# Five row tiles in the first norm instead of three, their weights' low parts by a subtraction on GpSimd instead of an accumulating DMA

## Chip, cores and metric

The kernel runs on one core of a Trainium2 chip. The metric is the device time of one execution in microseconds (us). Five engines work side by side, each in its own program order: TensorE (PE; PEld is its weight loading), VectorE (DVE), ScalarE (ACT), GpSimd (POOL) and SyncE (SP), which here only issues DMAs. ACT and POOL issue some DMAs too.

## What is computed

Two transformer blocks on 512 tokens of 1024 channels, all in float32. The part that matters here is the start of the first block, its first layer:

```python
mod = silu(c) @ ada_w[0] + ada_b[0]
shift, scale, gate = jnp.split(mod, 3, axis=-1)
h = rms_norm(x, norm_g[0]) * (1.0 + scale) + shift
z = h @ even_w_in                       # 1024 x 7296
a_val, a_glu, a_gate, r, k, v, wd, ad, b_gate = split_cols(z, EVEN_SIZES)
ya = conformer_conv(a_val, a_glu, ...) * silu(a_gate)
yb = rwkv7_mix(r, k, v, wd, ad, ...) * silu(b_gate)
x = x + gate * (concat(ya, yb) @ even_w_out)
```

After it come an attention layer, a short-convolution and pooling mixer, a layer with 16384 experts (choose the best 16 for each of 8 heads, then all experts' products), and a last gated projection.

## The kernel before

Channels lie on the 128 partitions, tokens along the free dimension: `x0` to `x7` are 128 x 512 tiles. A projection's output is worked in row tiles of 128 channels; `in_wev` holds 57 of them for `even_w_in`. Tile 48 is the low-rank inputs `wd` and `ad`, tiles 24 to 31 are `r`, 32 to 39 `k`, 40 to 47 `v`, 8 to 15 `a_glu`, 0 to 7 `a_val`.

To keep float32 accuracy each operand is split into a high and a low part, and `product` (L214 to L218) does three matmuls for each of the 8 pieces of 128 input channels: high x high (L216), high weight x low input (L217), low weight x high input (L218). A row tile is thus 24 matmuls into one PSUM bank. `weight` (L179) delivers the parts. In the first layer it loads a piece of 512 columns as `draw` (SP), copies it on ACT to `dh` (L190), copies it negated to `dl` (L191), and adds the same weights to `dl` by a second, accumulating DMA that POOL issues (L192). `draw` has 3 buffers, `dh` and `dl` 4.

`first_norm` (L313) makes `h`. The scales and shifts come from `in_adaT`: 16 loads `adaw` of 512 KB, each multiplied with `cond` and summed on DVE (L349), followed by small DVE instructions on `mod` and `gs` (L351, L352). For each j of 8, POOL makes `xr` = x times the reciprocal root mean square (L347), ACT applies scale and shift (L354) and makes the high part `xh` (L355), DVE the low part `xl` (L356), and PE adds the j-th three matmuls of every row tile in the tuple `FIRST` to its bank. When the norm ends, the tiles of `FIRST` lie complete in `self.ready`; `wev` hands them out, and projects any other tile with `proj`.

Behind it `even` runs the steps of `ORDER`: A0 A1 d c0 A2 B0 C0 B1 ... `A` (`rwkv_a`) makes the operands of two heads: ACT and DVE instructions on `r`, `k`, `v`, `sig`, `a`, `kk` up to `BK`, then 16 matmuls L620 and `MT`. `d` is the gate of the layer (`gate`, L423): 16 loads `pr` of 256 KB in two buffers, each reduced on DVE (L437). `c` is a convolution tile: 12 matmuls L774 whose operands use the buffers of `pr` again. `B` inverts small triangles: SP writes `MT` out as `Ld` (L647) and reads it back as `Lp` (L651), then 31 steps `Ltmp` (L660) and `Tp` (L662), then a transposition (L675) and matmuls L680. `C` is the recurrence over 8 chunks, each beginning with L702.

PSUM has 8 banks: `mm` 3 (two and one of `psum2`), `tp` 2, `xu` 2, `nb` 1. `xu` is used by `B` and `C`.

The order of instructions on each engine is set by a planner, the class `Order` (L1555): it has a price for each instruction, simulates the engines' queues by list scheduling from several priorities, and imposes the order that comes out shortest by its own prices on the whole program. A change at the start can thus move instructions everywhere. SP's loads in `first_norm` and of the gate are chained in the order in which they are written (`follow`).

Of the kernel before, what the change touches and what calls it, by code (L numbers as in the profile page):

```python
# [10 lines left out]
F32 = mybir.dt.float32  # L11
F32R = mybir.dt.float32r
# [7 lines left out]
T = 512  # L20
# [113 lines left out]
class Net:  # L134
# [178 lines left out]
    def first_norm(self, hi, lo):  # L313

        nc = self.nc
        mod, gs = self.mod[0], self.gs[0]
        with self.tc.tile_pool(name="ada", bufs=1) as pool:
            cond = pool.tile([128, 1024], F32, name="cond")
            loads = self.loads = []
# [7 lines left out]
                load(self.x[j], self.I["xT"][:, j])  # L327
            load(self.vec, self.I["vec"])
            def parts(i):
                for k in range(0, 1024, self.KR * 128):  # L330
                    yield from self.weight(self.I["wev"][i][:, k:k + self.KR * 128], loads)
            first = [(i, parts(i)) for i, _ in self.FIRST]
            ws = {}
            nc.scalar.activation(crow, crow, AF.Silu)
# [4 lines left out]
            rs = self.rstd(pool, self.x)  # L339
            self.ready = {i: self.bank(b) for i, b in self.FIRST}  # L340
            for j in range(8):
# [32 lines left out]
                                               op0=OP.mult, op1=OP.add)  # L374

    AW = 16
    FIRST = ((48, "mm"), (32, "mm"), (24, "mm"))
    WB, RB, KP, KR = 8, 6, 2, 2
    wd, DR, DB = None, 3, 4
    GB = 3  # L380
# [1520 lines left out]
```

## Time and profile before

| | us |
|---|---|
| median of 3 runs | 2843.48 (2837.21 to 2843.74) |
| the profiled execution | 2849.02 |
| its span, first to last instruction | 2847.1 |
| PE busy in the span | 2638.1 (93%) |
| DVE busy | 2125.0 (75%) |
| POOL busy | 1722.0 (60%) |
| ACT busy | 1467.5 (52%) |

The busy shares are averages over stages that have different limits. The first layer takes the first 780 us or so; the change touches its first 60 us directly. A row of the timeline begins with the start in us and the duration in us; what stands in brackets at its end is the engine's idle time before it and what ended that.

### The profile page before, as it was taken

The page shows a single profiled execution, that of the slowest core. Times are in us where ns is not written, and L with a number is a line of the kernel's source. Part 1 is how long each engine was busy: PE and PEld are TensorE (multiplying, and loading weights), DVE is VectorE, ACT ScalarE, POOL GpSimd, SP SyncE. Part 2 cuts the span into 40 slices and gives each one's busy share as a digit, 9 for nine tenths or more (in the row PEclk, how much of TensorE's full clock was granted, in tenths as well). Part 3 has the DMA queues.
Part 4 walks back from the last instruction along what each step waited for, and adds up shares of the span by engine and source line. Part 5 has one row for each costly group of instructions (what it writes and reads, how often), then busy time and mean ns, then how long its engine had stood idle before and what let it go on. Part 6 is the DMA issues. An engine that isn't in the chain of part 4 may idle for free.

```text
span 2847.1 us, 45547 instructions
## 1 busy us (share of the span) xinstructions
PE 2638.1 (93%) x14715; PEld 2209.6 (78%) x14715; DVE 2125.0 (75%) x4274; ACT 1467.5 (52%) x3135; POOL 1722.0 (60%) x1862
## 2 busy tenths in 40 slices
PE   5899999999979899999999978789999999999996
PEld 3666666666666678877888767789999999999995
DVE  6667657666459998963669999767787777788775
ACT  6646645557546348965453358533344334334435
POOL 4423512221255443346657688779999899898963
PEclk9879999999989999999999999989999999999998
DMA  8744444565783221223334366899999999999972
GB/s 268 163 91 95 96 103 104 108 136 128 174 284 98 69 80 51 77 72 107 94 106 133 112 194 248 309 327 333 319 333 330 331 327 327 326 320 337 328 244 77
DMA packets 353442, 552.26 MB, mean 194 GB/s; under 512 B 60081, under 2 KB 239153, under 8 KB 351538
## 3 DMA queue, kind: packets, MB, share of 16 engines
q1 hardware_dynamic: 224690, 295.22, 32.5%
q0 software_dynamic: 64800, 201.88, 23.9%
q10 hardware_dynamic: 63712, 52.24, 5.8%
q8 instruction: 116, 1.90, 0.3%
q14 instruction: 124, 1.02, 0.1%
HBM read 507.76 MB, written 41.42 MB: 193 GB/s over the span
## 4 chain that ended last, share of the span: by engine, by line
PE 59%; DVE 21%; DMA 6%; issue 5%; POOL 4%; ACT 3%; ACTq 0%; SPq 0%; DVEq 0%; POOLq 0%
PE mm L218 11%; PE mm L217 11%; PE mm L216 11%; PE xu L1254 2%; PE xu L1252 2%; PE xu L1253 2%; DVE x L778 2%; PE mm L774 2%; DVE o L1507 1%; DVE Ltmp L660 1%; DVE Tp L662 1%; PE tp L1254 1%; POOL wl L209 1%; PE tp L1253 1%; PE tp L1252 1%
## 5 line engine op out<-in xcount | busy, mean ns | idle before, releaser
L209 POOL TENSOR_TENSOR wl<-wraw,wh 128x256 fp32r<-128x256 f32 x937 | 759.3, 828 | 392.5 <-ACT wh L207 302.4
L207 ACT ACTIVATE wh<-wraw 128x256 fp32r<-128x256 f32 x937 | 368.3, 412 | 498.0 <-PE mm L217 256.7
L216 PE MATMUL mm<-xh,wh 128*128 128x352 f32 (+1 forms) x1464 | 512.2, 352 | 28.9 <-ACT wh L207 12.5
L218 PE MATMUL mm<-xh,wl 128*128 128x352 f32 (+1 forms) x1464 | 507.5, 351 | 13.7 <-POOL wl L209 13.4
L217 PE MATMUL mm<-xl,wh 128*128 128x352 f32 (+1 forms) x1464 | 509.6, 350 | 2.1 <-DVE xl L287 2.0
L216 PEld LDWEIGHTS mm<-xh,wh 128*128 128x128 f32 x1464 | 279.7, 191 | 53.0 <-ACT wh L207 15.9
L218 PEld LDWEIGHTS mm<-xh,wl 128*128 128x128 f32 x1464 | 278.6, 191 | 38.2 <-POOL wl L209 19.7
L217 PEld LDWEIGHTS mm<-xl,wh 128*128 128x128 f32 x1464 | 279.8, 191 | 23.0 <-DVE xl L287 4.5
L192 POOL DMA_DIRECT2D dl<-in_wev x114 | 100.9, 893 | 300.4 <-ACT dl L191 223.9
L1236 POOL TENSOR_TENSOR vl<-vraw,vh 128x1024 fp32r<-128x1024 f32 x96 | 232.3, 2421 | 5.6 <-ACT vh L1232 4.4
L1357 DVE SCALAR_TENSOR_TENSOR wide<-grow,gdot,wide 128x1024 f32<-128x1024 f32 x158 | 202.7, 1283 | 20.2 <-DMA grow<-in_ev,gidx 18.5
L1341 DVE SCALAR_TENSOR_TENSOR gscr<-grow,wide 128x1024 bf16<-128x1024 f32 x160 | 194.2, 1214 | 19.1 <-DMA grow<-in_ue,gidx 17.4
L216 PE MATMUL mm<-xh,dh 128*128 128x512 f32 x456 | 198.2, 437 | 10.6 <-ACT xh L355 10.0
L217 PE MATMUL mm<-xl,dh 128*128 128x512 f32 x456 | 194.1, 428 | 8.8 <-DVE xl L356 8.8
L218 PE MATMUL mm<-xh,dl 128*128 128x512 f32 x456 | 192.9, 425 | 6.0 <-DMA dl<-in_wev 6.0
L1326 POOL DMA_INDIRECT grow<-in_ue,gidx x160 | 163.6, 1022 | 56.3 <-issue 17.5
L1326 POOL DMA_INDIRECT grow<-in_ev,gidx x160 | 159.8, 999 | 39.6 <-issue 20.3
L1187 ACT ACTIVATE mm<-mm 128x352 f32<-128x352 f32 x96 | 43.0, 448 | 262.7 <-PE mm L218 257.7
L1254 PE MATMUL xu<-wwh,vl 128*128 128x352 f32 x512 | 167.2, 327 | 9.1 <-POOL vl L1236 9.1
L1252 PE MATMUL xu<-wwh,vh 128*128 128x352 f32 x512 | 166.1, 325 | 7.9 <-DVE x L1256 6.2
L1253 PE MATMUL xu<-wwl,vh 128*128 128x352 f32 x512 | 165.6, 324 | 0.0
L1232 ACT ACTIVATE vh<-vraw 128x1024 fp32r<-128x1024 f32 x128 | 134.4, 1053 | 50.3 <-DMA vraw<-in_ev 39.0
(573 smaller groups left out, 6762.8 us busy)
## 6 DMA issues: line engine op xcount, KB each, us to landing
vraw<-in_ev SPq DMA_DIRECT2D x128, 512.0 KB, 5.9
wraw<-in_uT SPq DMA_DIRECT2D x494, 128.0 KB, 4.5
draw<-in_wev SPq DMA_DIRECT2D x114, 256.0 KB, 3.2
dl<-in_wev POOLq DMA_DIRECT2D x114, 256.0 KB, 4.8
gs<-st SPq DMA_DIRECT2D x11, 2048.0 KB, 7.7
g<-gs ACTq DMA_DIRECT2D x32, 704.0 KB, 9.6
wraw<-in_wod SPq DMA_DIRECT2D x156, 128.0 KB, 2.2
adaw<-in_adaT SPq DMA_DIRECT2D x32, 512.0 KB, 7.2
```

Of the source, the lines that this page charges most:

```text
L207: nc.scalar.activation(wh, raw[:, s], AF.Copy)
L209: nc.gpsimd.tensor_tensor(wl, raw[:, s], wh.bitcast(F32), OP.subtract)
L216: nc.tensor.matmul(ps, wh, xh, start=start, stop=False)
L217: nc.tensor.matmul(ps, wh, xl, start=False, stop=False)
L218: nc.tensor.matmul(ps, wl, xh, start=False, stop=stop)
L1236: nc.gpsimd.tensor_tensor(l, raw, h.bitcast(F32), OP.subtract)
L1252: nc.tensor.matmul(po, vh[i][:, s], wh[i], start=(i == 0), stop=False)
L1253: nc.tensor.matmul(po, vh[i][:, s], wl[i], start=False, stop=False)
L1254: nc.tensor.matmul(po, vl[i][:, s], wh[i], start=False, stop=(i == len(wh) - 1))
L1326: self.nc.gpsimd.indirect_dma_start(out=t, out_offset=None, in_=src, in_offset=bass.IndirectOffsetOnAxis(ap=self.gidx[i][:, k:k + 1], axis=0))
L1341: nc.vector.scalar_tensor_tensor(scr, u, 1.0, x, op0=OP.mult, op1=OP.mult, accum_out=self.gdot[i][:, k:k + 1])
L1357: nc.vector.scalar_tensor_tensor(acc, r, w, acc, op0=OP.mult, op1=OP.add)
```

## The change

`FIRST` gets two more tiles, 40 (`v` of step A0) and 8 (`a_glu` of step c0), which accumulate in the two `xu` banks. The weights of all five are no longer delivered by `weight`, but in `first_norm` itself: a piece of 512 columns is loaded as `fraw`, ACT copies it to the high part `fh`, and POOL subtracts, `fl` = `fraw` - `fh`. Each of the three names has five buffers, so the second half of a tile's weights goes into the buffers of its first half. Ten loads take the place of six loads and six accumulating DMAs; ten copies on ACT that of twelve; ten POOL subtractions of 128 x 512 are new.

```diff
             def parts(i):
-                for k in range(0, 1024, self.KR * 128):
-                    yield from self.weight(self.I["wev"][i][:, k:k + self.KR * 128], loads)
+                for k in range(0, 1024, T):
+                    raw = pool.tile([128, T], F32, name="fraw", bufs=len(self.FIRST))
+                    load(raw, self.I["wev"][i][:, k:k + T])
+                    wh, wl = (pool.tile([128, T], F32R, name=n, bufs=len(self.FIRST)) for n in ("fh", "fl"))
+                    self.split(wh, wl, raw, nc.gpsimd)
+                    for c in range(0, T, 128):
+                        yield wh[:, c:c + 128], wl[:, c:c + 128]
...
-    FIRST = ((48, "mm"), (32, "mm"), (24, "mm"))
+    FIRST = ((48, "mm"), (32, "mm"), (24, "mm"), (40, "xu"), (8, "xu"))
```

`split` (L239) is the helper that was there: a copy on ACT and a subtraction on the engine given. Lines after L330 are five higher in the changed kernel.

On POOL, the stretch of the first norm up to the first instruction of step A0. Before:

```order
L192 DMA dl<-in_wev 128x512 x3
L347 ISA
L347 TENSOR_TENSOR xr<-x_76,rs 128x512
L347 TENSOR_TENSOR xr<-x_77,rs 128x512
L347 TENSOR_TENSOR xr<-x_78,rs 128x512
L347 TENSOR_TENSOR xr<-x_79,rs 128x512
L347 TENSOR_TENSOR xr<-x_80,rs 128x512
L347 TENSOR_TENSOR xr<-x_81,rs 128x512
L347 TENSOR_TENSOR xr<-x_82,rs 128x512
L192 DMA dl<-in_wev 128x512
L347 TENSOR_TENSOR xr<-x_83,rs 128x512
L192 DMA dl<-in_wev 128x512 x3
```

Now:

```order
L242 TENSOR_TENSOR fl<-fraw,fh 128x512 x5
L352 TENSOR_TENSOR xr<-x_76,rs 128x512
L352 TENSOR_TENSOR xr<-x_77,rs 128x512
L352 TENSOR_TENSOR xr<-x_78,rs 128x512
L352 TENSOR_TENSOR xr<-x_79,rs 128x512
L352 TENSOR_TENSOR xr<-x_80,rs 128x512
L352 TENSOR_TENSOR xr<-x_81,rs 128x512
L352 TENSOR_TENSOR xr<-x_82,rs 128x512
L352 TENSOR_TENSOR xr<-x_83,rs 128x512
L242 TENSOR_TENSOR fl<-fraw,fh 128x512 x5
L192 DMA dl<-in_wev 128x512 x4
```

Five subtractions stand ahead of the eight `xr` and five behind them, where accumulating DMAs stood.

On DVE, in step A0, from `sig` to `kk`. Before:

```order
L584 TENSOR_SCALAR sig<-sig 128x512
L592 SCALAR_TENSOR_TENSOR cu<-scan,sig 128x512
L593 TENSOR_TENSOR sig<-cu,sig 128x512
L546 SCALAR_TENSOR_TENSOR r<-mm,om,tm 128x512
L590 TENSOR_SCALAR rsq<-nb 128x512
L602 SCALAR_TENSOR_TENSOR kk<-k,vec,rsq 128x512
```

Now:

```order
L589 TENSOR_SCALAR sig<-sig 128x512
L597 SCALAR_TENSOR_TENSOR cu<-scan,sig 128x512
L598 TENSOR_TENSOR sig<-cu,sig 128x512
L442 SCALAR_TENSOR_TENSOR pr,gpart<-pr,cs 128x512
L442 SCALAR_TENSOR_TENSOR pr,gpart<-pr,crs 128x512
L595 TENSOR_SCALAR rsq<-nb 128x512
L551 SCALAR_TENSOR_TENSOR r<-mm,om,tm 128x512
L442 SCALAR_TENSOR_TENSOR pr,gpart<-pr,cs 128x512
L442 SCALAR_TENSOR_TENSOR pr,gpart<-pr,crs 128x512
L442 SCALAR_TENSOR_TENSOR pr,gpart<-pr,cs 128x512
L607 SCALAR_TENSOR_TENSOR kk<-k,vec,rsq 128x512
```

Five reductions of the gate stand between `sig` and `kk` (before there were two further up, ahead of this piece).

On SP, the loads around the first `Ld` (step B0). Before:

```order
L569 DMA wup<-in_wup 64x2x128 x2
L186 DMA draw<-in_wev 128x512
L434 DMA pr<-in_adaT 128x512 x2
L186 DMA draw<-in_wev 128x512 x2
L434 DMA pr<-in_adaT 128x512 x2
L647 DMA Ld<-MT 32x16x32 x2
L434 DMA pr<-in_adaT 128x512 x2
L651 DMA Lp<-Ld 32x1024 x4
```

Now:

```order
L439 DMA pr<-in_adaT 128x512 x6
L186 DMA draw<-in_wev 128x512 x3
L439 DMA pr<-in_adaT 128x512
L574 DMA wup<-in_wup 64x2x128 x2
L439 DMA pr<-in_adaT 128x512
L186 DMA draw<-in_wev 128x512
L439 DMA pr<-in_adaT 128x512 x4
L652 DMA Ld<-MT 32x16x32 x2
L439 DMA pr<-in_adaT 128x512 x2
L656 DMA Lp<-Ld 32x1024 x4
```

`Ld` stood behind 8 of the 16 loads of `pr` and stands behind 14.

## Rows read from the trace of the kernel before

**Rows 1.** Busy us (count) by stretch: PE, PEld, DVE, ACT, POOL; clock, DMA share, GB/s.

```profile
0.00:60.00 60.00, 31.72 (x82) 19.58 (x83) 43.81 (x87) 36.62 (x56) 26.21 (x39) 0.94 0.87 285
60.00:120.00 60.00, 44.35 (x201) 34.40 (x199) 41.33 (x85) 44.85 (x75) 27.86 (x45) 0.91 0.80 186
160.00:200.00 40.00, 39.75 (x256) 25.26 (x255) 29.21 (x77) 11.40 (x31) 5.95 (x10) 0.62 0.38 78
200.00:300.00 100.00, 97.16 (x591) 60.09 (x590) 58.86 (x147) 56.04 (x127) 28.34 (x47) 0.97 0.47 95
```

**Rows 2.** Waits from 0 to 60 us: us in total, times, longest.

```profile
PE mm L217 <- DVE xl L356: 8.8, 4, 6.0
DVE xl L356 <- ACT xh L355: 4.5, 3, 1.9
```

**Rows 3.** Timeline of PE: two neighbours at 53 us, two at 60 us.

```profile
52.94 0.63 PE L217 MATMUL mm<-xl,dh 128*128 128x512 f32 x1
53.37 0.63 PE L218 MATMUL mm<-xh,dl 128*128 128x512 f32 x1
...
60.55 0.39 PE L216 MATMUL mm<-xh,dh 128*128 128x512 f32 x1
60.78 0.39 PE L217 MATMUL mm<-xl,dh 128*128 128x512 f32 x1
```

**Rows 4.** Timeline of DVE in the first norm, ahead of and beside POOL's `xr`.

```profile
17.01 0.15 DVE L352 SCALAR_TENSOR_TENSOR gs<-mod,vec 128x1 f32<-128x1 f32 x1
...
18.55 1.22 DVE L349 SCALAR_TENSOR_TENSOR adaw<-adaw,cond 128x1024 f32<-128x1024 f32 x1
...
19.69 1.21 DVE L352 SCALAR_TENSOR_TENSOR gs<-mod,vec 128x1 f32<-128x1 f32 x1
...
20.93 2.27 DVE L349 SCALAR_TENSOR_TENSOR adaw<-adaw,cond 128x1024 f32<-128x1024 f32 x1
```

**Rows 5.** Tile `xr`: POOL's durations in ns (min/median/max), first and last start.

```profile
L347 POOL TENSOR_TENSOR xr<-x,rs x8: 1257/2017/2315, 19.2 to 33.6; 128x512 f32<-128x512 f32 x8
```

**Rows 6.** DMA queues from 0 to 60 us: packets, MB, share of 16 engines.

```profile
q1 hardware_dynamic: 6194, 15.00, 68.3%
q0 software_dynamic: 1008, 1.84, 17.3%
```

**Rows 7.** Timeline, step A0: DVE's `kk` and PE's first L620.

```profile
72.27 0.75 DVE L602 SCALAR_TENSOR_TENSOR kk<-k,vec,rsq 128x512 f32<-128x512 f32 x1 [4.89 <-ACT rsq L600]
...
79.04 2.32 PE L620 MATMUL tp<-AR,BK 64*128 64x128 f32 x16 [3.79 <-DVE BK L612]
```

**Rows 8.** Chain that ended last: start, us, what; waits for `pr`, three of five.

```profile
81.04 2.66 DMA pr<-in_adaT
...
84.52 6.17 DMA pr<-in_adaT
...
107.00 4.55 DMA pr<-in_adaT
```

**Rows 9.** Timeline, steps A1, c0, B0, C0: SP, PE, PE, DVE, PE, PE.

```profile
89.26 0.87 SPq L647 DMA_DIRECT2D Ld<-MT  x2
...
116.16 1.71 PE L620 MATMUL tp<-AR,BK 64*128 64x128 f32 x16
...
145.06 4.46 PE L774 MATMUL mm<-u,pr 128*128 128x512 f32 x10
...
158.22 0.87 DVE L675 STREAM_TRANSPOSE T<-Tt 32x256 f32<-32x256 f32 x2
...
162.93 1.09 PE L680 MATMUL xu<-T,MT 32*32 32x32 f32 x32
...
209.86 0.34 PE L702 MATMUL xu<-UV,MT 128*64 128x64 f32 x4
```

**Rows 10.** The choice of experts: busy us by stretch, and a wait from 1440 to 1860 us.

```profile
1520.00:1540.00 20.00, 20.00 (x110) 17.95 (x109) 20.00 (x104) 7.65 (x19) 15.71 (x19) 1.00 0.39 118
...
PE mm L216 <- ACT wh L207: 12.2, 3, 7.4
```

## The prediction

> **What bounds the kernel now.** I read the busy times by stage first. From 200 to 300 us PE is busy 97.16 of 100 us, and from 160 to 200 us 39.75 of 40, there at a granted clock of 0.62 on average [rows 1]: in the first layer PE sets the pace once it runs. In the first 60 us it is busy 31.72, in the next 60 us 44.35 [rows 1]: some 44 us in which it waits. The waits of the first norm come next: PE waits 8.8 us for `xl` from DVE, and DVE only 4.5 us in three waits for `xh` [rows 2]. So DVE's queue of scales paces the first norm. The timeline of DVE then shows what slows DVE there, and the chain of waits, from 80 us on, that the gate's `pr` loads pace steps A0 and A1 [rows 8]. The reader is to see two things: there is idle PE time to put work into, and DVE, which must feed that work, has none to spare.
>
> **Matmuls moved into the idle time.** Tiles 40 and 8 are 48 matmuls of 512 columns. Neighbours start 0.43 us apart at 53 us and 0.23 us apart at 60 us [rows 3]; this is the level of the clock. At the faster pitch 48 are 11.0 us. They stood behind the first norm, between 60 and 120 us. Counted in the orders of PE: ahead of A0's first L620 stood 122 of these matmuls and stand 175; ahead of A1's first L620 197 and 235; when c0's 12 convolution matmuls and A1's L620 are all issued, 240 and 240. So PE carries a lead of 53 matmuls (12.2 us) to A0 and of 38 (8.7 us) to A1, and at the end of c0 both kernels have done the same work. What counts is when that point is reached.
>
> **Subtractions on GpSimd.** Ahead of POOL's `xr` a small DVE instruction on `gs` takes 0.15 us and a sum over `adaw` 1.22 us; beside them the same take 1.21 and 2.27 us [rows 4]. Each loses 1.05 us to one POOL instruction, and POOL's own grow from 1.26 us (smallest) to 2.02 us (median) [rows 5]: the two engines go by turns. Eight `xr` make eight such stops. Ten subtractions of the same shape are added. The first two run before the first scales have landed and stop nobody; I take eight stops, 8.4 us, less about half of DVE's 4.5 us of waits [rows 2], which a later DVE shortens: the first norm ends 6 us later. Bounds: 0 (three stops, all absorbed by the waits) and 12 (ten stops and the 1.4 us by which scales land later, below).
>
> **DMA and ACT.** In the first 60 us the POOL queue's 1.84 MB, which are eight accumulating transfers, cost 17.3% of 60 us on all 16 engines, 1.30 us each; SP's 15.00 MB cost 68.3%, which is 0.72 us for 256 KB [rows 6]. Six accumulations less and four loads more are 4.9 us less DMA time. Nothing on the path waits for it, since DVE is short of time and not of scales; I count 0. In the other direction, five loads instead of three stand ahead of the first scales: at 0.72 us each, the scales land up to 1.4 us later (in the bound above). ACT does two copies fewer there; it is not the limit.
>
> **The gate's loads.** Now five reductions of `pr` stand between `sig` and `kk` on DVE. `pr` has two buffers, so each pair waits for a load that starts when the pair before is done; before, five such waits lay on the chain, 2.66, 6.17 and at last 4.55 us among them [rows 8], 4.4 us in the mean. Before, DVE was free for `kk` at 67.4 (72.27 less the 4.89 us of waiting for ACT [rows 7]), and `sig` was done 1.4 us ahead of that, at 66; now at 72. From there the first reduction (0.7), a load (4.4), the third (0.7), a load (4.4) and the fifth (0.7) make 10.9: `kk` at 82.9, 10.6 us later than 72.27, and A0's L620 at about 90 instead of 79.04 [rows 7]. Queued behind those reductions on DVE is all of A0, and PE's next L620. On SP `Ld` stands behind 14 loads of `pr` instead of 8: issued at about 101 instead of 89.26 [rows 9]. In return the gate is done some 6 us earlier than before, and A1's part on DVE no longer shares the queue with it: A1's L620 at about 123 instead of 116.16, only 7 later.
>
> **The end of c0.** Before, 43 products and the 12 convolution matmuls follow A1's first L620, and the last convolution ends at 149.5 [rows 9]. Now 5 products and 10 convolution matmuls follow. A convolution matmul shows as two records, 0.43 us each (4.46 us for ten overlapping ones [rows 9]): 8.5 us, with 16 matmuls L620 and the transpositions 15 us. That is 138, 11 us earlier, although everything on DVE is later.
>
> **B0 and C0.** B0 starts from `Ld`, so 12 us later. Its 31 steps on DVE and POOL took from 89 to 158 us [rows 9], twice what the steps need, because A1 and the gate stood between them. A good part of the 12 us closes: I take its end 5 us later (bounds 0 and 12). C0 follows: before, its last chunk began at 209.86 [rows 9]; now at 215, but by then 12 more convolution matmuls (10.2 us) and 4 more products (0.9 us) are done. 11 less 5 is **6 us gained**. After that PE is busy 97% [rows 1], so it keeps what it has.
>
> **Sum.** 2849.0 for the profiled execution (span 2847.1 and 1.9 around it) less 6 is 2843. The median of the runs, 2843.5, lies 5.5 below the profiled one, so on that footing 2837.5: I say **2838**.
>
> **The rivals.**
> *The lead is kept in full* (A). DVE's later end is taken up by its waits, and B0's steps close all of the 12 us. Then the 11 us at the end of c0 stay, with up to 3 more if the first norm is not late: 2843.5 - 11 to - 14, 2830 to 2833. For it: B0's chain was stretched by others. Against it: DVE shows hardly any idle time in the first norm.
>
> *The lock on DVE and the gate decide* (B, slower). The place is the first norm and `kk`: all ten subtractions stop DVE, the norm ends 12 us later, `kk` 16, `Ld` 18, and B0 hands all of it to C0, whose small matmuls run at the lower clock from 160 us on [rows 1] and must wait for DVE at each chunk. C0 then ends 18 us later with 11 us more done: 7 us lost, about 2851; with a further `pr` round or a slower clock 2855. It is a loss once C0's first L702 comes more than 11 us later than before. The Trainium skill, page "SBUF — State Buffer", section "Who interferes with whom", states that a VectorE instruction with two SBUF inputs and a GpSimd instruction that reads SBUF take turns at a lock held for the whole instruction, and that whoever is second waits in full. By that rule each of the ten subtractions would cost DVE 1.26 us, 12.6 us and not 6, and the total would be about 2844 to 2851; the trace agrees on the turns, with 1.05 us for each.
>
> *The planner's other changes decide* (C). It has reordered the whole program. In the choice of experts 231 dense products stand ahead of the first one-hot transposition on PE instead of 166, 65 of some 0.16 us by my estimate from the row of 20 us with 110 matmuls [rows 10], 10 us. DVE is full there (20.00 of 20) and PE later waits 12.2 us for weights [rows 10]. If the 65 fill waits, up to 10 us are gained; if they hold up DVE's pairs, as much is lost. I count 0 in the sum.
>
> *It doesn't do what it says* (D). The second half of `fh` and `fl` reuses the first half's buffers, so tiles 40 and 8 can only go on when their first four pieces are done; if most of the 48 matmuls slip behind the last `xl`, nothing has moved into idle time. The order of PE has 24 of the 120 products from the last `xh` on, against 19 of 72 before, which speaks against it. 2843 or so.
>
> **How the numbers follow.** Forecast 0.41, A 0.22, B 0.15, C 0.14 (0.08 gained, 0.06 lost), D 0.08. A measurement of this kernel can tell about 0.3%, 8.5 us, from no change. Faster by more: A, most of C's gains and the lower end of the forecast (0.06): 0.36. Slower by more: most of B and C's losses: 0.17. Within: 0.47. The range runs from A with a little of C, 2825, to B, 2852.
>
> **What would show it.** In the changed kernel: DVE's sums over `adaw` and the small instructions at 2.3 and 1.2 us beside `fl` as beside `xr`; the last `xl` at 60 us, not 54; `kk` of A0 behind waits for `pr`, at 82; A0's L620 at 90; `Ld` at 101; the last c0 convolution at 138; the last chunk of C0 at 215 and PE busy above 95% after that. Wrong would be: a last `xl` at 54 to 56 (stops cost nothing), or one past 64; c0 ending later than 149; a C0 later by more than 11; a layer that gains and a choice of experts that gives it back.

## The result, and the profile after

The changed kernel takes 2875.75 us (median of four runs, 2871.58 to 2883.67), the kernel before 2841.33 (four runs). The ratio is 1.0119, 95% interval 1.0098 to 1.014: some 34 us **slower**, where 2838 was forecast and 2852 was the upper end of the range. The profiled execution took 2873.45 (span 2871.5), 24.4 us more than the one before (span 2847.1). The two comparisons differ because the profiled execution before lies 5.5 us above its first median and after's 2.3 below its own.

Where the 24.4 us arise is read from five stage ends that both programs have, each the last (or first) instance of a row in the timelines:

| end of stage (last or first row) | before | after | stage longer by |
|---|---|---|---|
| first layer, last `xu<-UV,MT` of the recurrence | 735.0 | 752.3 | 17.3 |
| attention and mixer, last `poolw` product | 1428.9 | 1433.8 | -12.4 |
| choice of experts, first softmax step `top<-sel` | 1667.8 | 1700.4 | 27.7 |
| to the first expert product `xu<-wwh,vh` | 1877.1 | 1882.2 | -27.5 |
| end | 2847.1 | 2871.5 | 19.3 |

The change itself touches only the first of them. Such a difference, from one execution each, is good to some 5 us: a second execution of the changed kernel (`five_again`, below) ends the first layer at 757.1 and the mixer at 1437.0, against 752.3 and 1433.8. The busy times of the first layer, where the change lies, in the kernel after; the columns are those of [rows 1] (stretch and its length, then busy us and count of PE, PEld, DVE, ACT, POOL, then clock, DMA share, GB/s):

```profile
0.00:60.00 60.00, 32.72 (x93) 21.20 (x94) 46.48 (x79) 31.57 (x47) 34.27 (x24) 0.93 0.67 248
60.00:120.00 60.00, 44.77 (x175) 34.62 (x174) 34.32 (x68) 32.98 (x56) 18.08 (x40) 0.79 0.68 172
160.00:200.00 40.00, 36.35 (x216) 26.78 (x215) 36.47 (x89) 18.30 (x35) 15.85 (x26) 0.83 0.61 133
200.00:300.00 100.00, 94.57 (x645) 56.83 (x646) 67.11 (x164) 52.97 (x133) 25.72 (x43) 1.00 0.41 85
```

In the first 60 us PE is busy one microsecond more than in [rows 1], not eleven. From 60 to 120 us it is as busy as before (44.77 and 44.35 us), but the clock granted falls from 0.91 to 0.79, and fewer instructions get done (175 and 201). DVE is idle for 26 of those 60 us. In the norm itself the waits have hardly changed, from 0 to 60 us (us in total, times, longest; [rows 2] before):

```profile
PE mm L217 <- DVE xl L361: 8.1, 4, 3.1
DVE xl L361 <- ACT xh L360: 3.2, 2, 1.6
```

DVE's timeline after says where, the columns as in [rows 4]:

```profile
43.12 1.24 DVE L357 SCALAR_TENSOR_TENSOR gs<-mod,vec 128x1 f32<-128x1 f32 x1
44.35 2.33 DVE L354 SCALAR_TENSOR_TENSOR adaw<-adaw,cond 128x1024 f32<-128x1024 f32 x1
...
59.76 0.69 DVE L361 TENSOR_TENSOR xl<-xr,xh 128x512 fp32r<-128x512 f32 x1 [1.60 <-ACT xh L360]
68.69 2.35 DVE L498 TENSOR_SCALAR om<-vec 128x25 f32<-128x25 f32 x1 [8.24 <-PE xu L218]
...
71.19 0.75 DVE L551 SCALAR_TENSOR_TENSOR r<-mm,om,tm 128x512 f32<-128x512 f32 x1
...
87.74 0.75 DVE L607 SCALAR_TENSOR_TENSOR kk<-k,vec,rsq 128x512 f32<-128x512 f32 x1
```

The last `xl` ends the norm at 60, as forecast. Then comes a wait of 8.24 us that the prediction does not have: `om`, a tiny instruction on a constant (in before at 54.17, right behind the last `xl`), waits for PE. PE's timeline shows what for, the last product with `fl`, at 68.20; under it the later steps that answer to [rows 7, 9]:

```profile
68.20 0.39 PE L218 MATMUL xu<-xh,fl 128*128 128x512 f32 x1
97.74 2.39 PE L625 MATMUL tp<-AR,BK 64*128 64x128 f32 x16
...
133.11 1.81 PE L625 MATMUL tp<-AR,BK 64*128 64x128 f32 x8 [2.62 <-DVE BK L617]
...
155.32 1.02 PE L779 MATMUL mm<-u,pr 128*128 128x512 f32 x2
...
188.35 0.48 PE L707 MATMUL xu<-UV,MT 128*64 128x64 f32 x4
...
226.05 0.34 PE L707 MATMUL xu<-UV,MT 128*64 128x64 f32 x4
```

`om` reads nothing of `fl`. But `fl` is a tile of the pool "ada", which the first norm opens and closes, and the tiles of the next phase (`om`, `hb`, `ka`, `tm` and others) take over that memory. A0's first L625 comes at 97.74, 18.7 us later than in [rows 7], and C0's last chunk at 226.05 instead of 209.86 [rows 9].

The second place is the choice of experts. DVE's timeline after, ahead of the softmax:

```profile
1669.24 0.58 DVE L1477 TENSOR_REDUCE sel<-eq 128x64 f32<-128x256 bf16 x1
...
1680.98 1.22 DVE L1346 SCALAR_TENSOR_TENSOR gscr<-grow,wide 128x1024 bf16<-128x1024 f32 x1 [3.95 <-DMA grow<-in_ue,gidx]
...
1691.46 1.22 DVE L1346 SCALAR_TENSOR_TENSOR gscr<-grow,wide 128x1024 bf16<-128x1024 f32 x1 [9.25 <-DMA grow<-in_ue,gidx]
...
1697.27 1.22 DVE L1346 SCALAR_TENSOR_TENSOR gscr<-grow,wide 128x1024 bf16<-128x1024 f32 x1 [4.58 <-DMA grow<-in_ue,gidx]
...
1700.38 0.29 DVE L1487 COPY top<-sel 128x32 f32<-128x32 f32 x1 [1.88 <-ACT grep L1293]
```

The selection is done at 1669, as good as before (1666), but `top`, the first step of the softmax, stands behind row products whose gathers have not landed: 31 us later. In before it follows at 1667.84. The plan is a trade; PE's dense products are drawn forward. The windows of this stage, the one behind it and the rest, before:

```profile
1428.90:1667.80 238.90, 222.69 (x1145) 193.01 (x1144) 211.72 (x977) 104.06 (x247) 165.78 (x201) 0.98 0.40 123
1667.80:1877.10 209.30, 159.99 (x1078) 146.21 (x1078) 177.72 (x195) 135.56 (x353) 172.93 (x144) 0.94 0.76 274
1877.10:2847.10 970.00, 928.71 (x5604) 906.94 (x5602) 734.12 (x1084) 394.26 (x811) 821.38 (x781) 0.99 0.88 304
```

and after:

```profile
1433.80:1700.40 266.60, 251.24 (x1319) 221.97 (x1318) 218.94 (x1003) 117.12 (x282) 190.39 (x234) 0.98 0.43 132
1700.40:1882.20 181.80, 127.60 (x916) 118.35 (x914) 157.10 (x154) 124.96 (x324) 149.16 (x113) 0.90 0.74 270
1882.20:2871.50 989.30, 936.55 (x5596) 912.02 (x5596) 763.84 (x1099) 393.44 (x807) 816.97 (x778) 0.98 0.87 300
```

PE's timeline after, the first expert product:

```profile
1882.19 0.66 PE L1257 MATMUL xu<-wwh,vh 128*128 128x352 f32 x1 [27.31 <-ACT wwh L241]
```

PE does 174 more products in the first stage and 162 fewer in the next. So the two stages together come out even (448.2 and 448.4). But at 1854.9 PE has no product left ahead of the first expert product, which waits for its weights `wwh`, and stands idle for 27.31 us, and the rest of the program, with the same number of products (5596 and 5604), takes 19.3 us longer.

### The profile page after: what moved, and what is told of

Read it like the earlier page. It is cut to its first block, busy times and chain, and to the rows that moved or that the text cites. A ratio compares the mean times of both kernels' runs of the same rounds, so it can differ in the third digit from the quotient of the medians.

```text
span 2871.5 us, 45542 instructions
## 1 busy us (share of the span) xinstructions
PE 2639.3 (92%) x14715; PEld 2214.1 (77%) x14715; DVE 2159.4 (75%) x4274; ACT 1457.7 (51%) x3120; POOL 1736.7 (60%) x1862
## 3 DMA queue, kind: packets, MB, share of 16 engines
q14 instruction: 123, 1.01, 0.1%
## 5 line engine op out<-in xcount | busy, mean ns | idle before, releaser
L192 POOL DMA_DIRECT2D dl<-in_wev x104 | 91.6, 890 | 279.6 <-ACT dl L191 234.0
L216 PE MATMUL mm<-xh,dh 128*128 128x512 f32 x416 | 179.8, 433 | 9.9 <-ACT dh L190 3.6
L218 PE MATMUL mm<-xh,dl 128*128 128x512 f32 x416 | 176.8, 425 | 6.9 <-DMA dl<-in_wev 6.9
L217 PE MATMUL mm<-xl,dh 128*128 128x512 f32 x416 | 176.5, 425 | 0.0
```

What stands on the lines that cost most here:

```text
L216: nc.tensor.matmul(ps, wh, xh, start=start, stop=False)
L217: nc.tensor.matmul(ps, wh, xl, start=False, stop=False)
L218: nc.tensor.matmul(ps, wl, xh, start=False, stop=stop)
```

## The experiments

Every time below is a median of timed runs beside runs of the kernel before on the same chip; the executions of before had medians of 2841.9 to 2847.9. "Five" kernels have the five row tiles of the change, "three" kernels the three of before. The planner picks one plan for the whole program, so an edit can act through the instructions that it changes or through the plan that it draws. The experiments try to hold one or the other. That does not fully succeed: a kernel whose first norm is edited anew has a first layer planned anew, also where the late order is held.

### Is it the stage of the experts?

The changed kernel with the stage of the experts and all behind it issued in the relative order that the kernel before has:

```diff
-    nc = build(A, Order(build(A)).best()[1])
+    order = hold(base, base.best()[1], other, other.best()[1], cut, ocut)
+    nc = build(A, order, Net)
```

Here `base` is the changed program and `other` the one before; from the cut on, `hold` takes the sequence of `other`.

> The changed first norm as it is; but every instruction from the stage of the experts on (choice of experts, dense products, row gathers, the end) is issued in the relative order of the kernel before, on every engine. Nothing is left out. Theory R (the planner's other order at the choice of experts costs most of the loss: the softmax over the chosen scores, top<-sel on DVE, stands behind four row products that wait for their gathers and starts 32 us later than before): the time falls from 2876 to 2844 to 2850, top<-sel starts at about 1673, that is 5 after before's 1668, the first one-hot o<-iota,kt at about 1681. Theory F (the first layer's later end, 17 us at its last chunk, is what the end pays, and the order only moves with it): the time stays at 2865 to 2876. Either way the first layer is as in the changed kernel: A0's first transposes at 97.7, the last xu<-UV,MT of the even phase at 752.

2872.27 against 2847.08, 1.0082 (1.0048 to 1.0117). The three stages went back to the lengths of before:

```profile
1448.40:1688.10 239.70, 225.15 (x1149) 194.47 (x1148) 210.49 (x977) 103.99 (x248) 165.87 (x201) 0.98 0.40 122
1688.10:1897.00 208.90, 161.28 (x1079) 148.06 (x1078) 178.33 (x194) 134.07 (x350) 172.27 (x143) 0.94 0.76 270
1897.00:2871.60 974.60, 929.30 (x5603) 907.04 (x5602) 735.11 (x1085) 394.29 (x814) 822.14 (x782) 0.99 0.89 303
```

From the last `poolw` product to the end are now 1423.2 us (1437.7 in after, 1418.2 in before). In the profiled execution the first layer ended at 762.9, ten later than in after, in nearly the same order of instructions there (ACT issues 11 DMAs less in that stretch, and some of its instructions change places). The lengths of the stages are explained by the order, the total is not: it is still 25 us over before, and most of that lies ahead of them.

The mirror image, the kernel before with the late order of after (the same `hold`, `base` and `other` exchanged):

> The kernel before up to the stage of the experts, three row tiles by the accumulating DMA; from there every instruction in the relative order of the changed kernel. Nothing is left out. The mirror of the other run. Theory R: 2865 to 2872, top<-sel some 27 to 32 us later than before's 1668. Theory F: 2838 to 2845, the same as before.

2882.45 against 2847.08, 1.0146 (1.0093 to 1.0198). The three rows answer to those of after:

```profile
1441.80:1709.60 267.80, 251.06 (x1315) 221.13 (x1314) 221.15 (x1002) 116.19 (x282) 191.04 (x234) 0.98 0.43 132
1709.60:1891.30 181.70, 128.55 (x916) 119.75 (x914) 161.87 (x154) 124.26 (x324) 147.57 (x113) 0.90 0.74 270
1891.30:2876.20 984.90, 932.80 (x5596) 909.28 (x5596) 763.02 (x1099) 392.70 (x807) 819.91 (x778) 0.98 0.88 301
```

So after's late order lengthens these stages in a kernel that has no edit at all. The total is 35 us over before, though, more than either theory said: the last `poolw` product comes at 1441.8 instead of 1428.9, ahead of the order that was changed, and why is not known. To size the late order over all kernels of this study I take the time from the last `poolw` product to the start of ACT's last output tile `yo`. Where `top` follows the last `sel` (fourteen kernels, before with 1402.1 among them) it is 1398.8 to 1413.2. With after's late order it is 1420.7, 1423.7 (after a second time) and 1418.3 (this run). This run lies 16 us over before, and after 13 over the first run (1407.6), which differ in little but this order: some 13 to 16 us. Two other late orders, of kernels below, have 1459.7 and 1459.9.

The direct test, the softmax pulled forward in the kernel before under after's late order:

```diff
+    back = key[top] - sel - 15
+    for n in chain:
+        key[n] -= back
```

> The kernel before up to the stage of the experts; from there the order of the changed kernel, but the softmax over the chosen scores, the one-hots behind it and what they need are issued as early as the last chosen index allows, as a block; the rest (dense products, gathers) keeps its order around them. Nothing is left out. Theory R (the late softmax is what that order costs): top<-sel back within 5 us of the last sel<-eq, the total at 2838 to 2852. Theory S (the rest of that order, gathers issued later and dense products issued earlier, costs as much by itself): top<-sel early, but the total stays at 2860 to 2885.

2951.36, 1.0374 (1.0351 to 1.0397). The test failed: pulling forward what the chain needs moved other instructions too, and `top` still came 27 us behind the last `sel`, now waiting for ACT. Waits on `top` in this kernel (us in total, times, longest):

```profile
DVE top L1491 <- ACT grep L1297: 20.2, 1, 20.2
```

It says nothing on the question.

### Is it the memory of the first norm?

`fh` and `fl` in a pool of their own beside "ada", which the next phase does not take over. It has room for pieces of 384 columns. Late order of before, as in the first run:

```diff
-        with self.tc.tile_pool(name="ada", bufs=1) as pool:
+        with self.tc.tile_pool(name="ada", bufs=1) as pool, \
+             self.tc.tile_pool(name="fw", bufs=1, side="right") as fw:
...
-                    wh, wl = (pool.tile([128, T], F32R, name=n, ...
+                    wh, wl = (fw.tile([128, n], F32R, name=m, ...
```

> Five row tiles, subtracted on GpSimd, the stage of the experts held in the order of before; fh and fl (384 columns each, 15 subtractions in place of 10) lie in a pool of their own, on memory that only the convolution's pool takes over later, so that the mixing pool of A0 does not wait for the last product with fl. Nothing is left out. Theory P (the release of the first norm's pool is what A0 waits for: om<-vec at 68.7 waits 8.2 us for the last product): om<-vec starts right behind the last xl (about 60), r<-mm at 62 to 65 in place of 71.2, A0's first transposes at 88 to 92 in place of 97.7, the even phase ends 5 to 8 us earlier than in the run with the order held. Theory Q (the wait is for the products themselves: the two tiles more have to be finished first, and the pool is in no way late): om moves but r<-mm stays at 70 to 71 and A0's transposes at 96 to 98. Total 2838 to 2848 by either, since the attention phase took back 12 of 17 us in the changed kernel.

2864.89 against 2847.08, 1.0062 (1.0043 to 1.0082). DVE's timeline of this kernel at the end of the norm:

```profile
61.80 0.69 DVE L355 TENSOR_TENSOR xl<-xr,xh 128x512 fp32r<-128x512 f32 x1 [1.54 <-ACT xh L354]
62.58 2.35 DVE L503 TENSOR_SCALAR om<-vec 128x25 f32<-128x25 f32 x1
```

The wait of 8.24 us is gone: `om` follows the last `xl` at once. A0's first matmul into `tp` comes at 86.84, 10.9 earlier than in after, and the first layer ends at 744.5. The wait is real and this is its cause. What it is worth in the total is less clear: against the first run the median is 7.4 us lower, but the runs of the two overlap (2858.60 to 2874.13 and 2860.14 to 2883.34), and the first layer has another plan here, with two reductions of the gate between `sig` and `kk` instead of five. 17.8 us of loss remain.

### Is it the lock between DVE and GpSimd?

Five tiles, their low parts added by DMA as before, in the pool "ada"; late order of before:

```diff
-                    self.split(wh, wl, raw, nc.gpsimd)
+                    nc.scalar.activation(wh, raw, AF.Copy)
+                    nc.scalar.activation(wl, raw, AF.Copy, scale=-1.0)
+                    nc.gpsimd.dma_start(wl, self.I["wev"][i][:, k:k + T], accum_op=OP.add)
```

> Five row tiles, the low parts by the accumulating DMA again (ACT writes the negated high part, GpSimd's queue starts a DMA that adds the weights), in the same tiles of the first norm's pool; the stage of the experts held in the order of before. Nothing is left out. Theory G (GpSimd's subtractions stretch DVE's sums and the late xr, which puts the last xl from 53.3 to 59.8): the last xl is back at 53 to 55, the last product of the first norm at 63 to 66 in place of 68.6, A0's first transposes 4 to 6 us earlier than 97.7. Theory H (five accumulators by themselves make the norm end at 60): last xl stays at 58 to 61. The DMA queues carry 2.6 MB more in the first 60 us, which may put the last scales later by up to 7 us.

2862.43 against 2847.08, 1.0057 (1.0032 to 1.0082). The last `xl` comes at 59.2, no earlier than with the subtractions, and `om` waits 8.15 us as in after. SP's timeline shows the second load of scales of this kernel (start, then the time over which the eight are issued), and the waits from 0 to 60 us DVE's wait for ACT:

```profile
27.18 8.15 SPq L322 DMA_DIRECT2D adaw<-in_adaT  x8
DVE xl L355 <- ACT xh L354: 8.0, 3, 4.8
```

In after the loads start at 21.98 and end at 28.2, here at 35.3. DVE does not wait for these scales, however. It waits 8.0 us for `xh` (3.2 in after), the longest time, 4.8 us up to 48.9, while ACT makes eight copies for `fh` and `fl` in a row (from 43.2 on) ahead of the next `xh`. So each way delays the norm with five tiles: the subtractions take DVE's time, and with the accumulations, which need twice the copies on ACT, `xh` comes late.

The other half, three tiles, subtracted on GpSimd (`FIRST` as before, the rest as in after, late order of before):

> Three row tiles as before, their low parts subtracted on GpSimd in the first norm's pool; the stage of the experts held in the order of before. Nothing is left out. It takes the two tiles more out of the change. Theory P (the wait for the first norm's pool costs A0 most): om<-vec waits for the last product, r<-mm at 62 to 66 in place of 57.4, A0's first transposes at 84 to 90 in place of 79. Theory Q (the two tiles more cost it): r<-mm at 57 to 60, the transposes at 79 to 82. The last xl at 55 to 59, since six subtractions stand where ten did. Total within 2845 to 2860.

2862.17 against 2845.12, 1.0074 (1.0048 to 1.0099). The last `xl` is at 55.3 (53.34 before), two us late with six subtractions, and `om` waits in this kernel too, for less:

```profile
58.41 0.18 DVE L502 TENSOR_SCALAR om<-vec 128x25 f32<-128x25 f32 x1 [2.40 <-PE mm L218]
```

With five tiles PE has products left for eight us after the norm, with three for two. This kernel, too, has a first layer planned anew, so its 17 us are not the subtraction's alone.

### Is PE's lead worth anything?

The prediction's gain was matmuls taken away from the first layer's later part. Here 63 matmuls of tiles 40, 8 and 0 in the kernel before are narrowed to 2 columns, in the order of before:

```diff
-                self.product(ps, wh, wl, xh[k], xl[k], k == 0, k == kt - 1)
+                if less and self.LESS and k:
+                    self.product(ps[:, 0:2], wh, wl, xh[k][:, 0:2], xl[k][:, 0:2], k == 0, k == kt - 1)
```

> The kernel before, issued in its own order on every engine; of the weight products of the row tiles 40, 8 and 0 (A0's v and the two inputs of the first convolution) only those of the first eighth are full, the other 63 products take 2 of 512 columns. So 63 products of some 0.23 us lose most of their time, 5 to 10 us of TensorE's work go, and nothing that the chain of A0 (r, k, kk) waits for is later. It prices a lead on TensorE in the first layer when nothing pays for it. Theory L (the lead counts: the even phase is bound by TensorE, as step 5 of the prediction took it): the even phase's last product with MT moves from 735 to 739 down to 726 to 732. Theory W (the chain of A0, B0, C0 over DVE, ACT and the DMAs sets the phase, and TensorE's work is only cover): the last product stays at 733 to 740, and TensorE's idle time between 100 us and that end grows from 24 to 29 us to 31 to 38.

2844.55 against 2845.12, 0.9999 (0.9985 to 1.0013): no change. How much work is gone is read from PE's timeline of this kernel, neighbours among the narrowed products at either level of the clock:

```profile
106.40 0.25 PE L217 MATMUL mm<-xl,dh 128*128 128x2 f32 x1
106.51 0.25 PE L218 MATMUL mm<-xh,dl 128*128 128x2 f32 x1
...
124.65 0.35 PE L216 MATMUL mm<-xh,dh 128*128 128x2 f32 x1
124.86 0.35 PE L217 MATMUL mm<-xl,dh 128*128 128x2 f32 x1
```

They start 0.11 or 0.21 us apart, full ones 0.23 or 0.43 [rows 3]. By this estimate 63 narrowed products save 7 to 14 us; 21 of them lie ahead of 100 us. The profiled execution, the fastest of its runs, shows the first layer shorter:

```profile
100.00:720.60 620.60, 594.37 (x3788) 394.90 (x3787) 410.01 (x977) 363.06 (x793) 202.21 (x301) 0.97 0.53 113
```

against 635.00 us with 611.18 busy in before (the same stretch up to that stage's end):

```profile
100.00:735.00 635.00, 611.18 (x3786) 401.86 (x3784) 411.62 (x977) 362.65 (x793) 202.28 (x301) 0.95 0.52 111
```

That PE is busy 16.8 us less there is more than was taken away after 100 us. The clock has its part in it: this execution was granted 1.00 from 160 to 200 us,

```profile
160.00:200.00 40.00, 38.81 (x338) 25.36 (x338) 31.28 (x84) 17.02 (x47) 8.65 (x17) 1.00 0.52 107
```

where the one before had 0.62 [rows 1]. So the gain is there in one execution, and the median shows none of it. 7 to 14 us of PE's work gone, with no lock, no new wait and no new plan, shortened the total by 4 us at most (the lower end of the interval). One rival is left: the twelve runs were granted a mean clock of 0.968, those of before beside them 0.971, so the clock may have taken a part of the gain back.

### How much is it the plan?

First the changed kernel unaltered, a second time:

> The changed kernel itself, timed on the chip of these runs, so that the parts can be added up against it; nothing is changed. If the two parts (first layer, order of the choice of experts) add up, it lies 20 to 36 us over the kernel before of this chip, at 2867 to 2883.

2872.65 against 2845.12, 1.0114 (1.0079 to 1.0149): the same as at first, with the first layer ending at 757.1.

The planner tries list schedules from several weights and takes the cheapest by its own prices. The next kernels take another of its plans. The changed kernel with weight 100 (chosen: 200):

```diff
-    nc = build(A, Order(build(A)).best()[1])
+    nc = build(A, Order(build(A)).best(alphas=(100,))[1])
```

> The changed kernel, its planner held to the weight of 100, which is the weight whose plan it took for the kernel before (for the changed kernel it took 200, as 31 us shorter by its own prices: 2544 against 2575). Only the order of instructions differs; in this plan the softmax over the chosen scores follows the last chosen index at once, as before. No order is mixed from two plans. Theory R (the late softmax of the plan chosen costs about half of the loss, the first layer the other half): 2850 to 2864, top<-sel within 5 us of the last sel<-eq, the stage from there to the end 1160 to 1170 long. Theory N (the planner's prices are right about what this stage is worth, and the loss is the first layer's): 2870 to 2905.

2876.96 against 2844.26, 1.0113 (1.0084 to 1.0142). In this plan `top` follows the last `sel` by 1.7 us, and from the last `poolw` product to the last `yo` are 1398.8 us, as in before (1402.1). The total is not better, because the first layer is worse:

```profile
100.00:763.00 663.00, 625.10 (x3793) 413.05 (x3795) 430.26 (x993) 366.54 (x795) 201.26 (x301) 0.92 0.50 108
```

The same with the own place of `fh` and `fl` (`fw` as above):

> Five row tiles subtracted on GpSimd with fh and fl in memory of their own (384 columns each), planner held to 100, no order mixed from two plans. It takes the release of the first norm's pool and the late softmax out together. If both theories hold (pool and plan are the two parts of the loss) it lies 5 to 12 under the changed kernel with that plan, at 2843 to 2856, even with the kernel before or a little over it; A0's first transposes at 86 to 89. If the two tiles' lead counts for anything on TensorE once the norm ends only 8 us late, it would beat before: 2828 to 2840.

2860.39 against 2844.26, 1.0066 (1.0037 to 1.0094). Same chip and same weight, 16.6 us faster than the kernel above. The wait for the pool's memory is gone, but each of the two has drawn its own plan at that weight, so the 16.6 us are not the memory's alone. The profiled execution, the fastest of its runs, ended the first layer at 729.7:

```profile
100.00:729.70 629.70, 598.87 (x3781) 394.20 (x3781) 430.09 (x980) 365.19 (x794) 196.67 (x300) 0.97 0.51 110
```

Three tiles with the own place and GpSimd, and five tiles with it and accumulating DMAs, weight 100 both:

> The run with five tiles in memory of their own and the planner held to 100, cut back to three tiles (nine subtractions on GpSimd of 384 or 256 columns). Nothing else differs, nothing is left out. It measures the two tiles more by themselves, and beside before, GpSimd's subtraction by itself. Theory T (the two tiles are what is left of the loss: 40 products more ahead of A0, two more tiles of weights ahead of the scales): as fast as before, 2838 to 2850, the last xl at 54 to 57. Theory G (the subtraction on GpSimd, which stretches DVE's sums and the late xr, is what is left): 2855 to 2865, as with five tiles.

2869.6 against 2841.9, 1.0094 (1.0079 to 1.0109): no better than five, although the last `xl` (56.8) and A0 (81.9) are early.

> The same run with five tiles, memory of their own and the planner held to 100, but the low parts by the accumulating DMA in place of GpSimd's subtraction. Theory G: without GpSimd's subtractions the sums run at full speed and the kernel is back at 2838 to 2850. Theory T: 2855 to 2866, since the weights of five tiles, read twice, hold back the last scales: the last xl stays at 58 to 63.

2880.63 against 2841.9, 1.013 (1.0111 to 1.0149). In the first norm DVE waits for scales:

```profile
53.49 1.23 DVE L357 SCALAR_TENSOR_TENSOR adaw<-adaw,cond 128x1024 f32<-128x1024 f32 x1 [3.93 <-DMA adaw<-in_adaT]
...
63.25 0.69 DVE L364 TENSOR_TENSOR xl<-xr,xh 128x512 fp32r<-128x512 f32 x1 [1.60 <-ACT xh L363]
```

The loss is 38.7 us here and 16.1 with the subtraction: with the memory out of the way, the subtraction on GpSimd is the better of these two kernels for five tiles. How much of the gap is the plan that each has drawn is open.

Then the kernel before, without any edit, under three other plans: weight 200, weight 50, and weight 100 with one round less (`alphas=(200,)`, `alphas=(50,)`, `alphas=(100,), rounds=1`).

> The mirror: the kernel before, its planner held to the weight of 200, which was chosen for the changed kernel (by its prices 6 us longer than the plan it took, 2568 against 2562); in it the softmax stands 17 us behind the last chosen index. Nothing else differs. Theory R: 2855 to 2872, top<-sel 15 to 30 us behind the last sel<-eq. Theory N: 2838 to 2852, the same as before.

2930.81 against 2844.26, 1.0304 (1.0271 to 1.0337).

> The kernel before, unchanged but for the plan: the planner's weight is held to 50 (2575 by its own prices, against 2562 for the plan that before runs). It measures what another plan of the same program does, with no edit of the first norm at all. Theory Z (the planner's plans scatter on the chip by as much as the change lost, so that a part of the 33 us is the draw of a new plan and no part of the edit): 2855 to 2885, or below 2832. Theory E (plans of nearly the same price run alike, and the loss belongs to the edit): 2838 to 2853.

2878.61 against 2847.86, 1.0093 (1.0058 to 1.0129).

> The same with the weight of the plan that before runs, 100, but one round of refinement less (2578 by its prices); the softmax follows the last chosen index at once, as before. Theory Z: 2855 to 2885, or below 2832. Theory E: 2838 to 2853.

2869.2 against 2847.86, 1.0074 (1.0048 to 1.01).

By the planner's prices these three cost 6 to 16 us more than the plan of before (2561.9); the chip says 87, 31 and 21. The planner priced after's plan at 2544.4, 17.5 us *shorter* than before's. So each of the three new plans costs 20 us or more on the chip where nothing else changes, and the plan of before is better than all its neighbours that were tried. That suggests a theory, called Z in the expectations: the whole loss is the new plan, and the edit under the plan of before would cost nothing. The last two kernels test it. All instructions that both programs have (23,146 of 23,215) go in the order of before; the others stand where the changed kernel's plan has them, behind their neighbour:

```diff
-    nc = build(A, Order(build(A)).best()[1])
+    order = keep(base, base.best()[1], other, other.best()[1])
+    nc = build(A, order, Net)
```

> The changed first norm as it is (five tiles, GpSimd, first norm's pool), but every instruction that both kernels have is issued in the order of the kernel before, from the first norm to the end, as far as the waits for buffers allow; only the instructions that the edit adds or moves (48 products, the loads and the subtractions) stand where the changed kernel's plan puts them. So the edit is timed without the new plan. Theory Z (most of the 33 us is the new plan): 2840 to 2856. Theory E (most is the edit: the norm 6 us later, the wait for its pool, A0 18 us later): 2860 to 2880. By either, om<-vec still waits for the last product, at 66 to 69.

2892.48 against 2842.24, 1.0178 (1.0154 to 1.0201). Theory Z falls: in the order of before the edit costs 50 us, and with a plan of its own (after) 34. DVE's timeline behind the norm:

```profile
60.41 0.69 DVE L355 TENSOR_TENSOR xl<-xr,xh 128x512 fp32r<-128x512 f32 x1 [1.61 <-ACT xh L354]
67.22 1.26 DVE L502 TENSOR_SCALAR om<-vec 128x25 f32<-128x25 f32 x1 [6.12 <-PE mm L218]
74.10 0.69 DVE L446 SCALAR_TENSOR_TENSOR pr<-pr,cs 128x512 f32<-128x512 f32 x1 [5.59 <-DMA pr<-in_adaT]
```

The wait for the norm's memory is 6.12 us, and behind it DVE waits another 5.59 for a load of `pr`. `kk` comes at 89.3, C0's first chunk at 183.2, the first layer's end at 765.2 (+30). From the last `poolw` product on all goes as in before (1399.1 and 1402.1).

The same with the own place:

> The same with fh and fl in memory of their own (384 columns each), which takes the pool's wait out. Theory Z with a lead that counts: 2828 to 2842, faster than the kernel before. Theory Z with a lead that is only cover: 2840 to 2850. Theory E: 2852 to 2865.

2897.19 against 2842.24, 1.0196 (1.017 to 1.0222). `om` comes at 64.1, without the long wait, yet A0 at 94.8: an order in which a late load is waited for by PE in the old place (10.8 us for `wuh` in the kernel above, 7.5 in this one). Taking the wait away gains nothing in this pair. An order made for other arrival times does not fit, so the 50 us, too, are the edit's in a foreign order and not the edit's alone.

## Why the prediction was wrong, point by point

**Right.** The lock: beside `fl`, DVE's small instruction takes 1.24 us and the sum 2.33, the sizes of [rows 4], forecast 1.2 and 2.3. The norm's end: last `xl` at 59.76, forecast 60, 53.34 before. The eight further stops were right: 16 instructions of DVE are stopped instead of 8. The 6 us were partly luck, since three terms of the sum were off and made up for each other. The stops lose 16.0 us instead of 8.9, which is 7.1 more and not 8.4; the waits for `xh` shrink by 1.3 us (4.5 to 3.2) and not by 2.25; and the first sum starts 1.05 us later (15.57 instead of 14.52), which stood only in the bound. The Trainium skill's rule ("SBUF — State Buffer", "Who interferes with whom"), taken as ten whole subtractions, would have put it at 66 by estimate. Rival D did not happen: when the last `xl` is done, 88 of the 120 products have started (54 of 72 in before), so 34 of the 48 new ones are ahead of that point. That the other way of making the low parts ends it at 59 to 63 as well (runs by DMA above) was not seen. One slip had no weight: the DMA term, counted as 0, takes 1.84 MB for eight transfers, but they are seven of 256 KB, 1.48 us each, which makes 6.0 us less DMA time and not 4.9.

**The step that failed** is the one from the norm to `kk`. The prediction put `sig` at 72 because "before, DVE was free for `kk` at 67.4" and the norm ends six later. The step took it for granted that DVE runs on when the last `xl` is done. It does not: 8.24 us, `om` waiting for the last product with `fl`. In before the weights of the first norm lie in the long-lived buffers `dh` and `dl`; the change moves them into "ada", whose memory the next phase takes. The diff says so (`pool.tile` instead of `self.weight`), and the prediction put a price of 0 on it, without a word. `sig` was done at 80.2. The gate's loads, the term that was priced at 8.8 us, cost 2.7 (0.60, 0.50 and 1.60 in front of the last three reductions ahead of `kk`), since the reductions came 8 us later than forecast and the loads went on meanwhile. Three more reductions that the sum left out stand between `kk` and A0's first matmul. `kk` at 87.74 instead of 82.9, A0 97.74 instead of 90, A1 133.11 instead of 123, `Ld` at 108.79 instead of 101.

**The end of c0**, forecast 138, came at 156.3, later than before's 149.5. The forecast counted 15 us from an A1 at 123; A1 came ten later, and the rest took 23.2. In that rest PE did not wait at all, but it was granted 0.71 (columns as in [rows 1]):

```profile
133.10:156.30 23.20, 23.19 (x78) 15.07 (x79) 8.46 (x23) 9.45 (x19) 12.24 (x24) 0.71 0.51 115
```

In before the stretch from A1 to the end of c0 had 0.90. So the lead of PE went in two ways: ahead of A1 in waiting for DVE, ACT and loads (busy 55.27 of the 73.1 us from 60 on), and behind it in a slower clock, which the forecast's 15 us do not have.

**C0** decided. Rival B set its own point: a loss if C0's first L707 comes more than 11 us later than before. It came at 188.35 instead of 166.69, 21.7 later, and the last chunk at 226.05, forecast 215. PE's busy share from 200 to 300 was 94.57, under the 95 that the forecast asked for. The first layer ended 17.3 us later. Rival B had the right course, with the wrong mechanism (more stops, the norm 12 us late) and a price of 7 to 12.

**Rival C** happened as well, on its losing side: it was priced at up to 10 in either direction and counted as 0; the measured sum of the stages from the choice of experts on is 27.7 - 27.5 + 19.3 = 19.5. The 10 us rest on 0.16 us for a product, where the row that is given for it, 20 us over 110 matmuls, makes 0.18. The argument, "if the 65 fill waits, up to 10 us are gained", looked at the products moved forward and not at the softmax that they are traded for, nor at PE running dry at 1854.9. A planner that thinks 17.5 us are won is no evidence that they are.

**The gain itself** was not there to be had. Rival A's 11 us, and the 6 of the forecast, rest on PE time in the first layer being worth its length. With 7 to 14 us of it taken out and nothing added, the total moved by 4 us at most (0.9999, 0.9985 to 1.0013). That is another place than the lead of the forecast, so it is strong evidence and no proof.

**What stays open.** Three parts are shown as stages: the wait for the norm's memory (8.24 us on DVE), the late order (some 13 to 16 us), and a gain of 12.4 in attention and mixer that belongs to after's plan (679.9 in its second execution; other plans of the same edit, with stages of 702.3 and 702.4 us against 693.9, lose there). They do not add up to the total. Without the wait the total was lower by 7.4 and 16.6 us in two pairs and higher by 4.7 in the third, and with the late order of before it was still 25 us over before. Most of these kernels also have a plan of their own, and a new plan alone cost 21 us or more. What is not explained is why five tiles in their own place with a plan of their own still lose 16.1 us; their profiled execution, faster than the median, does not show it. A kernel near it, three tiles in their own place, suggests the clock more than waits. Its first layer:

```profile
100.00:751.90 651.90, 623.15 (x3800) 411.81 (x3798) 422.70 (x980) 367.01 (x796) 199.54 (x302) 0.93 0.49 108
```

PE is busy 12.0 us longer than in before's row (611.18, at 0.95) with 14 more products, and idle only 4.9 us longer (28.75 and 23.82). What makes the clock lower was not separated.

## What to carry to other kernels

When a tile moves to another pool, ask who takes that memory next: the next phase waits for the last reader of the old tiles, and a diff shows it only as a name. An engine's lead counts only if the engines that feed it keep up; where they do not, it turns into idle time further on. Under a global planner each edit draws a new plan, so time a few neighbouring plans of the unedited kernel first: here they lie 21 to 87 us above it, more than what the edit was to bring.

## What was not expected of the hardware

The granted clock goes with the total. Over 79 executions of the kernel before on these chips (2830.68 to 2857.62, median 2845.13) the correlation of span and mean granted clock is -0.68, some 18 us for each 0.01 of clock. Before's mean is 0.971; after had 0.963 to 0.966, the slowest plan (2930.81) 0.955. That is a correlation, and which comes first was not tested. Behind an idle stretch the rows show the lower level (1.2 GHz): from 1855.0 to 1882.2 PE is busy 0.01 us and the clock 0.54, and the next 47.8 us are granted 0.94, where before's first 52.9 us of that stage are granted 1.00. Idle time is not all of it: from 160 to 200 us PE was busy 39.75 of 40 us in the execution before and was granted 0.62 [rows 1], and in the narrowed kernel, busy 38.81, it was granted 1.00.
